# Branch D's gates as seven half-width products, convolution taps written behind weight chunks, an earlier layer norm and weight sums in four stretches

## The chip, the core and the metric

The kernel runs on one core of one Trainium2 chip. The metric is the device time of one execution in microseconds. A core has TensorE (PE, with its weight loads listed apart as PEld), VectorE (DVE), ScalarE (ACT), GpSimd (POOL) and SyncE (SP, which here only issues transfers); they run side by side and wait for one another through semaphores.

## The reference, cut to what matters

One layer over 512 time steps and 1024 channels, all in 32-bit floats. `h` is the normalised input; `z = h @ W_in` is cut into the inputs of four mixers and into four blocks of 1024 gate columns.

```python
y_sc   = (sc_b * causal_dwconv(sc_c * sc_x, sc_conv)) @ sc_out           # branch s
y_pool = pool_mixer(pool_in, pool_w, pool_scale)                         # branch p
y_conf = silu(layer_norm(causal_dwconv31(glu(conf_in)) + conf_b)) @ conf_out   # branch c
y_diff = diff_attention(q, k, v, ...) @ diff_out                         # branch d
x = x + (sum of sigmoid(gate_i) * y_i) @ w_o
x = x + conv_glu_ffn(rms_norm(x))                                        # 1024 -> 2 x 2816 -> 1024
```

`causal_dwconv31` is a depthwise convolution with 31 taps over 512 channels.

## The kernel before, in words

Activations lie channel-major: a tile holds 128 channels by 512 time steps. Every 32-bit operand is split into a high and a low part of the type fp32r, and a product is three matmuls: high by high, high by low, low by high (`mm3`). One 128x128 weight block with its three matmuls of 512 columns is a "unit".

**Weights** come in one stream of chunks through three buffers each of `raw`, `whi` and `wlo`. A plain chunk ("n" in `PLAN`) holds eight blocks, 128x1024; for each, SP issues one transfer, ACT casts the high part (L156) and DVE subtracts to get the low part (L157). `step` calls `load_chunk` for up to two chunks ahead of the one that the matmuls read. `state["unit"]` counts units; `at(u, f)` and `after(d, f)` run `f` when the count reaches a due unit, which places its instructions in the program order at that point. A planner then orders each engine's queue, except where `manual_schedule` keeps the order of the program; for POOL that holds throughout.

**Seven products** (`seven`, `products`): a 2x2 grid of weight blocks is multiplied by a pair of activation blocks with seven products of 256 columns in place of eight (each three matmuls). One such group of blocks takes a chunk of kind "s": three plain blocks from `wa` and four sums of blocks from `sums`, 896 columns in all, in two transfers. The sums are made on the fly by POOL's accumulating transfers in DRAM (`make_sums`, four transfers for each group of four chunks, each waiting for the one before). The activation side is prepared by `fold`, once per pair of channel tiles. Four PSUM banks hold the results; two ACT copies and four DVE adds turn them into the outputs (L702 to L715).

**Order of the work.** The convolution's inputs (chunks 0 to 7), q, k, v (8 to 19), branch s's and p's inputs with attention between them as timed events, then s outputs and gates, p outputs and gates (up to chunk 56). Branch d then has for each of eight tiles an output product (`mixed`, 4 units, tile `yd`) and a gate (`gate`, 8 units, tile `gtd`): the first four (`STD = 4`), then the four gate pairs of branch c in seven products each (tiles `gc0` to `gc6`, kept in `gates`), then the other four. Branch c's outputs (`yc`) follow with their merges, then `w_o`, then the feed-forward layer in two parts: ten up-projected tiles and a down projection in seven products (`dn0x`), then twelve and another (`dn1x`).

The 124 taps (L402, L405, tile `cacc`) are events spread from 32 to 560 units after the first time-major product. The layer norm (`norm_mean`, `norm_center` `MULAG` units later, `norm_out` `VARLAG` units after that) begins before the last gate pair of branch c. The weight sums come in three calls: groups 0 to 2 with k's heads, 3 to 6 after the pool inputs, 7 to 14 after the last gate of branch c.

Of the kernel before, what the change touches and what calls it, by code (L numbers as in the profile page):

```python
# [9 lines left out]
F32 = mybir.dt.float32  # L10
# [23 lines left out]
UPC = CW // P  # L34
AHEAD = 2
STEP = 13
TAP0 = 32
TAP1 = 560
VLAG = 8
OLAG = 13  # L40
WARM = 8
# [4 lines left out]
SW = 4 * P  # L46
SUMU = 30
EARLY = 3
MIDDLE = 7
DEEP = 2  # L50
ENDS = 3
STD = 4
FOLD = 4
FOLDS = 14
FOLD0 = -26
MULAG = 22
VARLAG = 14
PLAN = [("n", 57 + 3 * STD // 2)]
PLAN += [("s", MP * FOLD), ("n", 3 * (KD - STD) // 2 + 4 + 8 + 2 * CUT), ("s", MP * CUT // 2), ("n", 2 * (NP - CUT)), ("s", MP * (NP - CUT) // 2)]
LOG_EXP = "natural_log_exp_and_others"  # L60
START = 2
PIECES = 4
PLAG = 20
NLAG = 11
ALAG = 6
HP = 0
SQ0 = 8
NTMP = 12
SQS = 4
# [20 lines left out]
def hybrid_layer_kernel(ctx: ExitStack, tc: tile.TileContext, xT: bass.AP, w: bass.AP, cols: bass.AP, wa: bass.AP,  # L90
# [12 lines left out]
    def bank(name):  # L103
        return psum.tile([P, T], F32, tag="bank", name=name)

    def t2(name, dt=F32):
        return tmp.tile([P, TW], dt, tag="tmp", name=name)[:, :T]

    def m2(name, dt=F32R):
        return mid.tile([P, T], dt, tag="mid", name=name)  # L110
# [11 lines left out]
    sums = [dram.tile([P, GRP * SW], F32, name=f"sums{g}") for g in range(n_of["s"] // GRP)]  # L122

    fetched = []

    def fetch(i, pieces=1):
        kind, c = plan[i]
        raw = wp.tile([P, CW], F32, tag="raw", name=f"wr{i}", bufs=3)
        if kind == "s":
            g, o = divmod(c, GRP)  # L130
            n = AW + SW
            nc.sync.dma_start(raw[:, :AW], wa[c])
            nc.sync.dma_start(raw[:, AW:n], sums[g][:, o * SW:(o + 1) * SW])
            return ((slice(0, n), raw[:, :n]),)
        cuts = [slice(i * CW // pieces, (i + 1) * CW // pieces) for i in range(pieces)]
        for s in cuts:
            nc.sync.dma_start(raw[:, s], w[c][:, s])
            if pieces > 1 and s.start == 0:
                nc.sync.dma_start(xt[0], xT[0])
        return tuple((s, raw[:, s]) for s in cuts)  # L140

    def load_chunk(pieces=1, between=None):
        c = len(chunks)
        while len(fetched) <= min(c + (DEEP if plan[c][0] == "s" else 0), len(plan) - 1):
            if len(fetched) > c and plan[len(fetched)][0] == "n":
                break
            fetched.append(fetch(len(fetched)))
        hi = wp.tile([P, CW], F32R, tag="whi", name=f"wh{c}", bufs=3)
        lo = wp.tile([P, CW], F32R, tag="wlo", name=f"wl{c}", bufs=3)
        with tc.high_priority(HP):  # L150
            for cut, raw in fetched[c]:
                n = (cut.stop - cut.start) // pieces
                for i in range(pieces):
                    s = slice(cut.start + i * n, cut.start + (i + 1) * n)
                    src = raw[:, i * n:(i + 1) * n]
                    nc.scalar.copy(hi[:, s], src)  # L156
                    nc.vector.tensor_tensor(out=lo[:, s], in0=src, in1=hi[:, s].bitcast(F32), op=ALU.subtract)  # L157
                if between and cut.start == 0:
                    between()
        chunks.append((hi, lo))  # L160

    events = []
# [2 lines left out]
    def at(u, f):  # L165
        events.append((u, len(events), f))
        events.sort(key=lambda e: e[:2])
# [89 lines left out]
    def col(name, i=0, n=1):  # L257
        o = COLS[name] + i
        return gains[:, o:o + n] if o < NG else colt[:, o - NG:o - NG + n]
# [9 lines left out]
    def raw_in(k):  # L269
        raw.append(split(xt[k], f"raw{k}", scale=col("mix_norm", k)))  # L270

    nc.scalar.dma_start(gains, cols[:, :NG])
    fetched.append(fetch(0, PIECES))
    nc.scalar.dma_start(xt[1], xT[1])
    fetched.append(fetch(1))
# [68 lines left out]
    def conf_glu(j, pa, pg):  # L344
# [3 lines left out]
        nc.vector.tensor_tensor(out=g, in0=g, in1=rs, op=ALU.mult)  # L348
        nc.vector.tensor_tensor(out=glus[j][:, CK - 1:], in0=pa, in1=g, op=ALU.mult)

    first = [bank(f"ca{i}") for i in range(4)]
    def input_norm():
        ps = bank("ss1")
# [38 lines left out]
        conf_glu(j, pa, pg)  # L392
    for k in range(KD):
        after(NLAG * k, lambda k=k: norm(k))

    acc31 = [None] * 4

    def tap(j, i):
        wc = col("conf_conv", j * CK + i)
        if i == 0:  # L400
            acc31[j] = m2(f"cacc{j}", F32)
            nc.vector.tensor_scalar(  # L402
                out=acc31[j], in0=glus[j][:, :T], scalar1=wc, scalar2=col("conf_b", j), op0=ALU.mult, op1=ALU.add)
        else:
            nc.vector.scalar_tensor_tensor(  # L405
                out=acc31[j], in0=glus[j][:, i:i + T], scalar=wc, in1=acc31[j], op0=ALU.mult, op1=ALU.add)

    def time_major(name):
        pss = [bank(f"{name}{t}") for t in range(4)]
# [51 lines left out]
    nc.vector.tensor_reduce(out=lam2, in_=lamt, op=ALU.add, axis=AX.X)  # L461
    lam = const.tile([P, 1], F32, name="lamc")

    taps = [(j, i) for j in range(4) for i in range(CK)]
    u1, u2 = state["unit"] + TAP0, state["unit"] + TAP1
    for n, (j, i) in enumerate(taps):
        at(u1 + (u2 - u1) * n // len(taps), lambda j=j, i=i: tap(j, i))
    qrows = qk_norm("q", time_major("q"))
    qT, kT = [], []
    after(QLAG, lambda: qT.extend(qk_heads("q", qrows, qg)))  # L470
# [244 lines left out]
        nc.vector.tensor_tensor(out=s5_, in0=p2[:, :H], in1=s5_, op=ALU.add)  # L715
        return p1[:, H:], p3[:, H:], p3[:, :H], s5_

    def gate_pair(m, name, keep=False):
        c11, c12, n21, n22 = seven(f"g{name}{m}", hops)
        gs = [m2(f"sg{name}{m + i}", F32) if keep else t2(f"sg{name}{m + i}") for i in range(2)]  # L720
        for g, c, x, scale in (
                (gs[0], right, c11, 1.0), (gs[0], left, c12, 1.0), (gs[1], right, n21, -1.0), (gs[1], left, n22, -1.0)):
            nc.scalar.activation(g[:, c], x, AF.Sigmoid, scale=scale)
        return gs

    def gate(m, name, keep=False):
        pg = bank(f"gt{name}{m}")
        project(pg, h)
        g = m2(f"sg{name}{m}", F32) if keep else t2(f"sg{name}{m}")
        nc.scalar.activation(g, pg, AF.Sigmoid)  # L730
        return g

# [13 lines left out]
    def mixed(m, name, act):  # L746
        py = bank(f"y{name}{m}")
        project(py, act)
        return py
# [7 lines left out]
        py = mixed(m, "p", [ypool[m // 2]])  # L757
        merge(m, py, gate(m, "p"), scale=col("pool_scale", m))
    ydiff = [(od[0][:, i, :], od[1][:, i, :]) for i in range(HEADS)]
    for m in range(STD):  # L760
        py = mixed(m, "d", ydiff)
        merge(m, py, gate(m, "d"))
    yconf = []
    gates = []

    def norm_mean():
        t = t2("cm")
        nc.vector.tensor_tensor(out=t, in0=acc31[0], in1=acc31[1], op=ALU.add)
        for j in (2, 3):
            nc.vector.tensor_tensor(out=t, in0=t, in1=acc31[j], op=ALU.add)  # L770
        after(MULAG, lambda a=tsplit(t, "mu"): norm_center(a))
# [14 lines left out]
            nc.scalar.activation(a, a, AF.Silu, scale=col("ln_g", j), bias=col("ln_b", j))  # L786
            yconf.append(split(a, f"yc{j}"))

    for m in range(0, KD, 2):
        if m == KD - 2:  # L790
            while events:
                events.pop(0)[2]()
            norm_mean()
        gates += gate_pair(m, "c", True)
    turn = sm.tile([P, 1], F32, tag="turn", name="turn", bufs=1)
    nc.gpsimd.tensor_copy(turn, gates[-1][:, :1])
    make_sums(MIDDLE, len(sums))
    for m in range(STD, KD):
        py = mixed(m, "d", ydiff)
        merge(m, py, gate(m, "d"))  # L800
    for m in range(KD):
        merge(m, mixed(m, "c", yconf), gates[m], last=True)

    x1 = []
    for m in range(KD):
# [60 lines left out]

    parts = ((0, CUT), (CUT, NP))
    for part, (p0, p1) in enumerate(parts):
        ops, free, even = [], list(homes), None
        last = [hs[:, k, j, :] for k in range(KD) for j in (0, 1)]  # L870
        for p in range(p0, p1):
            g = ffn_up(p)
            if p % 2:
                ops.append(operands(p // 2, even, g, last if p == NP - 1 else free))
            even = g
        for m in range(MP):
            y0, y1 = x1[2 * m], x1[2 * m + 1]
            o0, o1 = (y0, y1) if part == 0 else (t2(f"outa{m}"), t2(f"outb{m}"))
            if part and m == MP - 1:
                seven_last(f"dn{part}{m}", ops, y0, y1, o0, o1,  # L880
                           lambda i, c, q: q.dma_start(out[2 * m + i][:, c], (o0, o1)[i][:, c]))
                continue
            c11, c12, n21, n22 = seven(f"dn{part}{m}", ops)
            for o, y, c, z, op in (
                (o0, y0, right, c11, ALU.add), (o0, y0, left, c12, ALU.add),
                (o1, y1, right, n21, ALU.subtract), (o1, y1, left, n22, ALU.subtract)):
                nc.vector.tensor_tensor(out=o[:, c], in0=y[:, c], in1=z, op=op)
            if part:
                for i, o in enumerate((o0, o1)):
                    for c in (right, left):  # L890
                        nc.sync.dma_start(out[2 * m + i][:, c], o[:, c])


def _layout(x, mix_norm, w_in, sc_conv, sc_out, pool_w, pool_scale, conf_conv, conf_conv_b, conf_ln_g, conf_ln_b,
# [39 lines left out]
    for m in range(KD):  # L934
        parts.append(pw[m // 2][:, (m % 2) * P:(m % 2 + 1) * P])
        gate_of(1, m)
    for m in range(STD):
        tile_of(do, m)
        gate_of(3, m)
    for m in range(STD, KD):  # L940
        tile_of(do, m)
        gate_of(3, m)
    for m in range(KD):
        tile_of(co, m)
    for m in range(KD):
# [4 lines left out]
    stream = np.concatenate(parts, axis=1)  # L950
    w = np.ascontiguousarray(stream.reshape(P, -1, CW).transpose(1, 0, 2))

    pairs = [(win, 36 + 2 * 8 + m, k) for m in range(0, KD, 2) for k in range(FOLD)]
    for k0, k1 in ((0, CUT // 2), (CUT // 2, NP // 2)):
        pairs += [(dn, m, k) for m in range(0, KD, 2) for k in range(k0, k1)]

# [53 lines left out]
```

## Time and profile before

| | |
|---|---|
| median of 3 runs | 877.63 us (876.4 to 877.92) |
| profiled execution | 875.85 us, of which 874.1 us is the span from the first to the last instruction |
| TensorE | 4514 matmuls, busy 868.5 us (99%), granted clock 0.999 |
| VectorE | 686.3 us (79%) |
| ScalarE | 415.7 us (48%) |
| transfers | 143.68 MB, 164 GB/s on the mean |

Busy time is the time covered by an engine's instructions. Matmuls are pipelined and overlap in the records, so the pace of TensorE is read from the distance between starts.

### The profile page before, as it was taken

The numbers are of one execution on the slowest core, as the hardware profiler recorded it, in microseconds if no ns is written. First come the engines' busy times: TensorE is split into PE (matmuls) and PEld (weight loads), VectorE is DVE, ScalarE is ACT, GpSimd is POOL, SyncE is SP. The second block draws the span as 40 slices with busy tenths as digits, with TensorE's granted clock in tenths as the row PEclk, the third lists the DMA queues.
The fourth block names the chain that finished last, engine by engine and source line by source line (L and its number), as shares of the span: only waits on it lengthen the run. The fifth ranks groups of instructions, "written<-read, shape, count | busy, mean of one in ns | idle before, by whom it ended". The sixth has DMA issues, their size and how long they took to land.

```text
span 874.1 us, 12008 instructions
## 1 busy us (share of the span) xinstructions
PE 868.5 (99%) x4514; PEld 742.4 (85%) x4514; DVE 686.3 (79%) x1099; ACT 415.7 (48%) x624; POOL 85.9 (10%) x114
## 2 busy tenths in 40 slices
PE   9999999999999999999999999999999999999998
PEld 7888888888888888899888888888899888888998
DVE  7299976897867997998778566988876788888856
ACT  7243355464666434335574345444454344444532
POOL 1003301102411100000011011111000000000000
PEclk9999999999999999999999999999999999999999
DMA  7333377762398784347779887879876422223573
GB/s 263 112 97 97 121 180 207 183 142 97 126 223 199 177 201 123 111 125 210 208 195 244 214 207 210 216 212 208 172 198 188 125 101 97 97 99 88 160 227 119
DMA packets 64842, 143.68 MB, mean 164 GB/s; under 512 B 5536, under 2 KB 31136, under 8 KB 64544
## 3 DMA queue, kind: packets, MB, share of 16 engines
q1 hardware_dynamic: 40112, 99.26, 35.0%
q0 software_dynamic: 24240, 43.26, 25.3%
q8 instruction: 35, 0.57, 0.3%
q10 hardware_dynamic: 432, 0.40, 0.1%
q14 instruction: 23, 0.19, 0.1%
HBM read 140.80 MB, written 45.35 MB: 213 GB/s over the span
## 4 chain that ended last, share of the span: by engine, by line
PE 97%; DVE 1%; DMA 1%; issue 0%; ACT 0%; SPq 0%; DVEq 0%
PE fg L197 14%; PE fu L197 14%; PE gts L197 5%; PE gtd L197 5%; PE wo L197 5%; PE gtp L197 5%; PE c L197 3%; PE pi L197 3%; PE x L197 3%; PE ys L197 3%; PE k L197 2%; PE yd L197 2%; PE b L197 2%; PE v L197 2%; PE yc L197 2%; PE q L197 2%
## 5 line engine op out<-in xcount | busy, mean ns | idle before, releaser
L156 ACT CAST wh<-wr 128x1024 fp32r<-128x1024 f32 (+2 forms) x189 | 188.2, 998 | 231.6 <-issue 30.1
L157 DVE TENSOR_TENSOR wl<-wr,wh 128x1024 fp32r<-128x1024 f32 (+2 forms) x189 | 219.6, 1165 | 68.8 <-ACT wh L156 61.5
L197 PE MATMUL fg<-hs,wh 128*128 128x512 f32 x352 | 108.4, 389 | 0.0
L197 PE MATMUL fu<-hs,wh 128*128 128x512 f32 x352 | 108.4, 389 | 0.0
L405 DVE SCALAR_TENSOR_TENSOR cacc<-glu,colt,cacc 128x512 f32<-128x512 f32 x120 | 89.8, 748 | 2.3
L197 PEld LDWEIGHTS fu<-hs,wh 128*128 128x128 f32 x352 | 66.1, 188 | 13.8
L197 PEld LDWEIGHTS fg<-hs,wh 128*128 128x128 f32 x352 | 66.0, 188 | 13.7
L830 DVE SCALAR_TENSOR_TENSOR fc<-f,colt,fc 128x512 f32<-128x512 f32 x88 | 65.8, 749 | 7.4 <-ACT fc L828 6.3
L197 PE MATMUL fg<-hs,wl 128*128 128x512 f32 x176 | 68.5, 389 | 0.0
L197 PE MATMUL fu<-hs,wl 128*128 128x512 f32 x176 | 68.5, 389 | 0.0
L828 ACT ACTIVATE fc<-f,colt 128x512 f32<-128x512 f32 x44 | 31.6, 718 | 19.1 <-DVE f L114 16.6
L197 PE MATMUL gts<-hs,wh 128*128 128x512 f32 x128 | 40.0, 394 | 0.0
L197 PE MATMUL gtd<-hs,wh 128*128 128x512 f32 x128 | 39.4, 389 | 0.0
L197 PE MATMUL gtp<-hs,wh 128*128 128x512 f32 x128 | 39.4, 389 | 0.0
L197 PEld LDWEIGHTS fg<-hs,wl 128*128 128x128 f32 x176 | 33.0, 188 | 6.8
L197 PEld LDWEIGHTS fu<-hs,wl 128*128 128x128 f32 x176 | 33.1, 188 | 6.8
L825 DVE TENSOR_TENSOR f<-fu,rs 128x512 f32<-128x512 f32 x22 | 15.1, 688 | 20.3 <-PE fu L197 20.3
L242 POOL DMA_DIRECT2D sums<-s x15 | 15.2, 1013 | 141.1 <-DMA sums<-s 141.1
L197 PEld LDWEIGHTS gts<-hs,wh 128*128 128x128 f32 x128 | 23.7, 188 | 5.5 <-issue 0.7
L197 PEld LDWEIGHTS gtd<-hs,wh 128*128 128x128 f32 x128 | 24.0, 188 | 5.0
L197 PEld LDWEIGHTS gtp<-hs,wh 128*128 128x128 f32 x128 | 24.0, 188 | 5.0
L505 ACT ACTIVATE p<-p,st 128x128 f32<-128x128 f32 (+3 forms) x32 | 17.7, 555 | 16.9 <-DVE st L502 16.8
(1685 smaller groups left out, 2131.6 us busy)
## 6 DMA issues: line engine op xcount, KB each, us to landing
wr<-w SPq DMA_DIRECT2D x124, 512.0 KB, 3.6
sums<-s POOLq DMA_DIRECT2D x15, 1024.0 KB, 9.5
wr<-sums SPq DMA_DIRECT2D x60, 256.0 KB, 3.8
wr<-wa SPq DMA_DIRECT2D x60, 192.0 KB, 3.0
sums<-s POOLq DMA_DIRECT2D x15, 512.0 KB, 7.0
sums<-s POOLq DMA_DIRECT2D x15, 256.0 KB, 4.8
x<-xT SPq DMA_DIRECT2D x8, 256.0 KB, 3.8
xin<-xT SPq DMA_DIRECT2D x1, 1024.0 KB, 8.1
```

What stands on the lines that cost most here:

```text
L156: nc.scalar.copy(hi[:, s], src)
L157: nc.vector.tensor_tensor(out=lo[:, s], in0=src, in1=hi[:, s].bitcast(F32), op=ALU.subtract)
L197: nc.tensor.matmul(ps, a[i], b[j], start=start and n == 0, stop=stop and n == 2, skip_group_check=shared)
L242: lambda g: nc.gpsimd.dma_start(view(g, 2, 4), src(s2, g, 2), accum_op=ALU.add),
L405: nc.vector.scalar_tensor_tensor(out=acc31[j], in0=glus[j][:, i:i + T], scalar=wc, in1=acc31[j], op0=ALU.mult, op1=ALU.add)
L505: nc.scalar.activation(p[:, :n], p[:, :n], AF.Exp, bias=st[:, m:m + 1], scale=-1.0, accum_out=st[:, 2 + m:3 + m])
L825: nc.vector.tensor_tensor(out=u[:, 2:2 + T], in0=ps, in1=rs, op=ALU.mult)
L828: nc.scalar.activation(c, u[:, 2:2 + T], AF.Copy, scale=col("ffn_conv", o + 2))
L830: nc.vector.scalar_tensor_tensor(out=c, in0=u[:, i:i + T], scalar=col("ffn_conv", o + i), in1=c, op0=ALU.mult, op1=ALU.add)
```

## The change

Branch d's eight gates are computed by `gate_pair` as branch c's are, four pairs in seven products each; `hops`, the folded activations, serve both. For each pair of tiles of d and then of c, the order is now: gate pair, two output products, two merges. `STD`, the kept gates and their eight tiles are gone. The plan has 76 "s" chunks (60 before) and 117 "n" chunks (125 before), so 19 groups of sums (15 before).

The taps are no longer events: `load_chunk` for chunks 9 to 50 runs under `manual_schedule` on DVE and appends `TAPS[c]` taps behind the chunk's low part. The folds are due 38 units earlier. `norm_mean` is called once the pool branch's products are written, ahead of branch d. Weight sums: groups 0 to 2 and 3 to 7 where the first two calls were, 8 to 12 after the last merge of branch c, 13 to 18 when the first down projection has written `x1[7]`. At the start, the small `gains` transfer and the first input tile swap their queues.

```diff
-TAP0 = 32
-TAP1 = 560
...
-MIDDLE = 7
+MIDDLE = 8
+LATE = 13
...
-STD = 4
...
-FOLD0 = -26
+FOLD0 = -64
...
-PLAN = [("n", 57 + 3 * STD // 2)]
-PLAN += [("s", MP * FOLD), ("n", 3 * (KD - STD) // 2 + 4 + 8 + 2 * CUT), ("s", MP * CUT // 2), ("n", 2 * (NP - CUT)), ("s", MP * (NP - CUT) // 2)]
+PLAN = [("n", 57)] + 2 * MP * [("s", FOLD), ("n", 1)]
+PLAN += [("n", 8 + 2 * CUT), ("s", MP * CUT // 2), ("n", 2 * (NP - CUT)), ("s", MP * (NP - CUT) // 2)]
+TAPS = dict(zip(range(9, 51), (
+    5, 0, 4, 6, 3, 0, 2, 6, 1, 0, 4, 1, 2, 2, 4, 2, 4, 2, 3, 5, 5, 3, 3, 2, 3, 4, 3, 3, 5, 0, 0, 0, 2, 4, 5, 2, 2, 4, 4,
+    6, 5, 3)))
...
             if pieces > 1 and s.start == 0:
-                nc.sync.dma_start(xt[0], xT[0])
+                nc.sync.dma_start(gains, cols[:, :NG])
...
-        with tc.high_priority(HP):
+        with ExitStack() as order:
+            if c in TAPS:
+                order.enter_context(tc.manual_schedule(engines={mybir.EngineType.DVE}))
...
+            for _ in range(TAPS.get(c, 0)):
+                tap(*taps.pop(0))
...
-    nc.scalar.dma_start(gains, cols[:, :NG])
+    nc.scalar.dma_start(xt[0], xT[0])
...
-    u1, u2 = state["unit"] + TAP0, state["unit"] + TAP1
-    for n, (j, i) in enumerate(taps):
-        at(u1 + (u2 - u1) * n // len(taps), lambda j=j, i=i: tap(j, i))
...
-    for m in range(STD):
-        py = mixed(m, "d", ydiff)
-        merge(m, py, gate(m, "d"))
...
-    for m in range(0, KD, 2):
-        if m == KD - 2:
-            while events:
-                events.pop(0)[2]()
-            norm_mean()
-        gates += gate_pair(m, "c", True)
-    turn = sm.tile([P, 1], F32, tag="turn", name="turn", bufs=1)
-    nc.gpsimd.tensor_copy(turn, gates[-1][:, :1])
-    make_sums(MIDDLE, len(sums))
-    for m in range(STD, KD):
-        py = mixed(m, "d", ydiff)
-        merge(m, py, gate(m, "d"))
-    for m in range(KD):
-        merge(m, mixed(m, "c", yconf), gates[m], last=True)
+    norm_mean()
+
+    def more_sums(x, g0, g1):
+        turn = sm.tile([P, 1], F32, tag="turn", name=f"turn{g0}", bufs=1)
+        nc.gpsimd.tensor_copy(turn, x[:, :1])
+        make_sums(g0, g1)
+
+    for name, act in (("d", ydiff), ("c", yconf)):
+        for m in range(0, KD, 2):
+            gs = gate_pair(m, name)
+            for i in (m, m + 1):
+                merge(i, mixed(i, name, act), gs[i - m], last=name == "c")
+    more_sums(merged[-1][0].bitcast(F32), MIDDLE, LATE)
...
     for part, (p0, p1) in enumerate(parts):
+        if part:
+            more_sums(x1[KD - 1], LATE, len(sums))
...
-    pairs = [(win, 36 + 2 * 8 + m, k) for m in range(0, KD, 2) for k in range(FOLD)]
+    pairs = [(win, 36 + br * 8 + m, k) for br in (3, 2) for m in range(0, KD, 2) for k in range(FOLD)]
```

## Rows read from the trace of the kernel before

**Rows 1.** The page: busy time, share and instructions of each engine; chain by engine.
```profile
PE 868.5 (99%) x4514; PEld 742.4 (85%) x4514; DVE 686.3 (79%) x1099; ACT 415.7 (48%) x624; POOL 85.9 (10%) x114
PE 97%; DVE 1%; DMA 1%; issue 0%; ACT 0%; SPq 0%; DVEq 0%
```
**Rows 2.** All waits of TensorE in the span: us, times, longest.
```profile
PE warm L282 <- DVE zeros L279: 1.5, 1, 1.5
PE ca L197 <- ACT raw0h L224: 0.5, 1, 0.5
```
**Rows 3.** Timeline of TensorE: start us, length us, engine, line, operation, tiles, count.
```profile
358.37 0.62 PE L197 MATMUL gtd<-hs,wh 128*128 128x512 f32 x2
...
363.81 0.62 PE L197 MATMUL yd<-od,wh 128*128 128x512 f32 x2
...
380.13 0.40 PE L197 MATMUL gc0b<-at,wh 128*128 128x256 f32 x2
...
390.20 0.40 PE L197 MATMUL gc2b<-at,wh 128*128 128x256 f32 x2
```
**Rows 4.** Windows: length; busy us (instructions) of PE, PEld, DVE, ACT, POOL; clock; DMA.
```profile
46.46:138.54 92.08, 92.08 (x433) 76.45 (x431) 80.27 (x131) 39.88 (x62) 18.85 (x13) 1.00 0.48 138
138.54:247.37 108.83, 108.83 (x537) 88.44 (x535) 92.94 (x187) 61.98 (x118) 23.25 (x24) 1.00 0.58 151
247.37:303.97 56.60, 56.60 (x267) 46.82 (x266) 41.22 (x68) 30.70 (x50) 7.30 (x9) 1.00 0.83 198
379.98:420.28 40.30, 40.30 (x337) 40.26 (x336) 36.20 (x49) 22.72 (x38) 0.00 (x0) 1.00 0.61 183
```
**Rows 5.** Windows of the taps alone (L405): length, DVE busy (instructions), clock, DMA.
```profile
46.46:138.54 92.08, 22.49 (x30) 1.00 0.48 138
138.54:247.37 108.83, 22.37 (x30) 1.00 0.58 151
247.37:303.97 56.60, 15.30 (x21) 1.00 0.83 198
```
**Rows 6.** Groups of instructions by line and shape: count, busy us, mean ns, idle before.
```profile
L157 DVE TENSOR_TENSOR wl<-wr,wh 128x1024 fp32r<-128x1024 f32 x123 | 151.7, 1234 | 39.4 <-ACT wh L156 32.6 <-PE ss L336 6.3
L157 DVE TENSOR_TENSOR wl<-wr,wh 128x896 fp32r<-128x896 f32 x60 | 65.1, 1089 | 26.3 <-ACT wh L156 25.8
L714 DVE TENSOR_TENSOR gc0r<-gc0c,gc0q 128x512 f32<-128x512 f32 x1 | 0.7, 685 | 0.0
```
**Rows 7.** Timeline of ScalarE in the layer norm.
```profile
435.97 0.69 ACT L315 ACTIVATE rlv<-var,epsc 128x512 f32<-128x512 f32 x1 [2.86 <-PE var L337]
...
443.16 1.05 ACT L156 CAST wh<-wr 128x1024 fp32r<-128x1024 f32 x1 [1.18 <-PE gtd L197]
...
452.34 1.05 ACT L156 CAST wh<-wr 128x1024 fp32r<-128x1024 f32 x1
```
**Rows 8.** Timeline of POOL: first, 29th and last of the third call's 32 transfers.
```profile
424.73 0.53 POOL L240 DMA_DIRECT2D sums<-s  x1
...
607.24 0.90 POOL L240 DMA_DIRECT2D sums<-s  x1
...
634.50 1.01 POOL L243 DMA_DIRECT2D sums<-s  x1 [8.06 <-DMA sums<-s]
```
**Rows 9.** Timelines of DVE and SP: `x1[7]` after `dn0`; the last group's first fetch.
```profile
682.14 0.42 DVE L887 TENSOR_TENSOR x<-x,dn03s 128x256 f32<-128x256 f32 x1
...
850.07 0.32 SPq L133 DMA_DIRECT2D wr<-sums  x1
```
**Rows 10.** The page, transfers: count, size, median us from issue to landing.
```profile
wr<-sums SPq DMA_DIRECT2D x60, 256.0 KB, 3.8
...
sums<-s POOLq DMA_DIRECT2D x15, 256.0 KB, 4.8
```
**Rows 11.** Timeline of ScalarE at the start.
```profile
4.92 0.72 ACT L224 ACTIVATE raw0h<-xin,gains 128x512 fp32r<-128x512 f32 x1 [1.11 <-DMA xin<-xT]
...
8.17 1.14 ACT L156 CAST wh<-wr 128x512 fp32r<-128x512 f32 x2 [0.97 <-DMA wr<-w]
```

More of the change, by code (lines that the diff above doesn't have):

```diff
@@ L65 @@
 ALAG = 6
-HP = 0
 SQ0 = 8
@@ L124, in hybrid_layer_kernel @@
     fetched = []
+    taps = []
     def fetch(i, pieces=1):
@@ L349, in conf_glu, with tap @@
         nc.vector.tensor_tensor(out=glus[j][:, CK - 1:], in0=pa, in1=g, op=ALU.mult)
+    acc31 = [None] * 4
+    def tap(j, i):
+        wc = col("conf_conv", j * CK + i)
+        if i == 0:
+            acc31[j] = m2(f"cacc{j}", F32)
+            nc.vector.tensor_scalar(
+                out=acc31[j], in0=glus[j][:, :T], scalar1=wc, scalar2=col("conf_b", j), op0=ALU.mult, op1=ALU.add)
+        else:
+            nc.vector.scalar_tensor_tensor(
+                out=acc31[j], in0=glus[j][:, i:i + T], scalar=wc, in1=acc31[j], op0=ALU.mult, op1=ALU.add)
+    taps += [(j, i) for j in range(4) for i in range(CK)]
     first = [bank(f"ca{i}") for i in range(4)]
@@ L394, in hybrid_layer_kernel @@
         after(NLAG * k, lambda k=k: norm(k))
[L396 to L406, printed above, removed]
     def time_major(name):
@@ L462, in hybrid_layer_kernel @@
     lam = const.tile([P, 1], F32, name="lamc")
-    taps = [(j, i) for j in range(4) for i in range(CK)]
-    u1, u2 = state["unit"] + TAP0, state["unit"] + TAP1
-    for n, (j, i) in enumerate(taps):
-        at(u1 + (u2 - u1) * n // len(taps), lambda j=j, i=i: tap(j, i))
     qrows = qk_norm("q", time_major("q"))
@@ L716, in seven, with gate_pair @@
         return p1[:, H:], p3[:, H:], p3[:, :H], s5_
-    def gate_pair(m, name, keep=False):
+    def gate_pair(m, name):
         c11, c12, n21, n22 = seven(f"g{name}{m}", hops)
-        gs = [m2(f"sg{name}{m + i}", F32) if keep else t2(f"sg{name}{m + i}") for i in range(2)]
+        gs = [t2(f"sg{name}{m + i}") for i in range(2)]
         for g, c, x, scale in (
@@ L724, in gate_pair, with gate @@
         return gs
-    def gate(m, name, keep=False):
+    def gate(m, name):
         pg = bank(f"gt{name}{m}")
         project(pg, h)
-        g = m2(f"sg{name}{m}", F32) if keep else t2(f"sg{name}{m}")
+        g = t2(f"sg{name}{m}")
         nc.scalar.activation(g, pg, AF.Sigmoid)
@@ L759, in hybrid_layer_kernel @@
     ydiff = [(od[0][:, i, :], od[1][:, i, :]) for i in range(HEADS)]
-    for m in range(STD):
-        py = mixed(m, "d", ydiff)
-        merge(m, py, gate(m, "d"))
     yconf = []
-    gates = []
     def norm_mean():
@@ L936, in _layout @@
         gate_of(1, m)
-    for m in range(STD):
+    for m in range(KD):
         tile_of(do, m)
[L939 to L942, printed above, removed]
     for m in range(KD):
```

## The prediction

> **What bounds the kernel now.** I read the page first: TensorE is busy 99% of the span and 97% of the chain that ended last is TensorE [rows 1]. Busy time alone proves little for a pipelined engine, so I read its waits next. In the whole span TensorE waits for another engine twice, both times in the first six microseconds [rows 2]. The reader should see that no wait is left to remove: only fewer or shorter matmuls can make this kernel faster, and any new wait makes it slower at full price. The timeline then gives the two paces. One gate of 24 matmuls of 512 columns runs from 358.37 to 363.81, 5.44 us, so 0.2267 us a matmul. One pair in seven products, 84 matmuls of 256 columns, runs from 380.13 to 390.20, 10.07 us, so 0.120 us a matmul [rows 3]. The windows show the clock at 1.00 throughout, its 2.4 GHz level, and how full the other engines are while TensorE never pauses [rows 4].
>
> **The matmuls.** Four pairs of branch d's gates change form. A pair cost 2 x 5.44 = 10.88 us and will cost 10.07 us [rows 3]: 0.81 us saved, 3.24 us for four. The saving is small because the matmul count rises from 48 to 84 and half the columns cost 53% of the time. The `yd` and `yc` products, the two layer norm sums and everything else on TensorE are only reordered. This term is exact as long as the pace of the `gc` stage holds when two plain products follow each pair.
>
> One rule speaks against this term. The Trainium skill, page "TensorE: Matmul & The Clock Gate", section "Back-to-back issue gap", puts a sustained stream of weight load and matmul at about 81 ns for 128 columns and 131 ns for 512. A straight line between them, an estimate, gives 98 ns for 256, hence 84 x 98 = 8.2 us against 48 x 131 = 6.3 us a pair: four pairs would lose 7.8 us instead of gaining 3.2. This trace does not agree, with 227 and 120 ns in this kernel's own type, and I go by the rows.
>
> **The weights.** Eight plain chunks become sixteen of kind "s". VectorE has 16 x 1.089 - 8 x 1.234 = 7.6 us more to subtract [rows 6], ScalarE a similar amount to cast, SP 24 more transfers to issue. Each pair also gets an epilogue, about 3 x 0.685 + 0.42 = 2.5 us of VectorE. What hides it: branch c's four pairs, back to back, leave VectorE 36.20 of 40.30 us busy and ScalarE 22.72, taps among it, without a wait of TensorE [rows 2, 4]. In the new order a pair with its two plain products lasts 10.07 + 5.44 = 15.5 us, and VectorE needs in it 4 x 1.089 + 1.234 + 2.5 + four merge operations at about 0.685 = 10.8 us. Price 0; without that cover each microsecond VectorE falls behind, past the two chunks of lead, is one of TensorE's.
>
> **The taps.** All 124 now sit behind chunks 9 to 50. A chunk is loaded when the matmuls reach the one two before it, so I map `TAPS` on the windows: 42 fall in 46 to 139 us, 47 in 139 to 247, 35 in 247 to 304. Now there are 30, 30 and 21 (and one first tap in each, of L402, which I leave as it is); VectorE does 57.8, 70.6 and 25.9 us without them [rows 4, 5]. With 41, 46 and 34 at 22.49 / 30 = 0.75 us the new load is 88.5 of 92.1, 105.1 of 108.8 and 51.4 of 56.6 us. It fits, with 3% to 9% to spare. What is queued behind a tap is the next chunk's low part, for which TensorE waits. From 304 us on VectorE has no taps at all, which makes room for the earlier folds. Bounds: 0, and 4.3 us if VectorE's operations come out 6% longer in the first two windows (193.6 x 0.06 = 11.6 us, of which 7.3 are to spare). I take 0, since the sums stay under the time in all three.
>
> **The layer norm.** `norm_mean` moves ahead of branch d. `norm_center` falls 22 units later, at the end of the first pair; `norm_out` runs at the first step 14 units after that, the plain products of the second pair. Branch d begins 10.88 us (two products of 2.72, one gate) before 358.37 [rows 3], at 347.5, so that is about 347.5 + 15.5 + 10.1 = 373 us. Before, that work fell on plain chunks of 5.44 us each. There ScalarE needed from 435.97 past 452 us for the norm, and between two weight casts 9.2 us went by, from 443.16 to 452.34 [rows 7]. Now this stretch runs into the third pair's seven products, where a chunk lasts 10.07 / 4 = 2.52 us and two chunks of lead are 5.0 us. Bounds: 0 if the planner slips the casts between the activations, 9.2 - 5.0 = 4.1 us if the casts stay as far apart. I take 0.3 us, nearer to nothing: the windows show that this engine has spare time in such a stage (22.72 of 40.30 us, [rows 4]), and branch c does not need the norm until its first output product, at 347.5 + 4 x 15.5 + 10.1 = 420 us.
>
> **The weight sums.** Four more groups, 16 POOL transfers. The second call now makes five groups in place of four, and nothing behind it on POOL is urgent. The third call, after the merges at 347.5 + 8 x 15.5 = 471.5, makes five by 471.5 + 5 x 26.1 = 602 (pitch below), and the first down projection begins eight `w_o` products and ten tiles later, at 471.5 + 28 x 5.44 = 624. The fourth is the close one. Six groups start when `x1[7]` is written, 682.56 before [rows 9], 679.3 with 3.24 us saved. Seven groups took 607.24 - 424.73 = 182.5 us, 26.1 us each, and the eighth took 634.50 - 607.24 plus a landing of 4.8, 32 us [rows 8, 10]. So the last of six lands at about 679.3 + 5 x 26.1 + 32.1 = 842 us. Its first chunk, fourth from the end of the 24, is fetched at 850.07 - 3.2 = 846.8 [rows 9]. SP issues in order, so a late group holds back every fetch and store behind it. The margin is 5 us, and what the two chunks ahead in the buffers give beyond it. Price 0, bounds 0 to 8 us (each of the five groups 10% slower, 13 us, less the margin).
>
> By the Trainium skill, page "DMA: Bandwidth & Descriptors", section "Anatomy of one DMA", a POOL transfer takes 2 us plus its bytes at 436 GB/s: an estimate of 15 us for a group, and no danger at all. The rows show 26, so I keep the risk.
>
> **The start.** The first matmul waits for `raw0h`, which waited 1.11 us for its input [rows 11]; its transfer now goes first on ACT's queue. That can bring at most 1.1 us, or cost some tenths if `gains`, now second on SP, is late. But ScalarE's next casts wait for a later weight transfer at 8.17 [rows 11], which sits behind the same bytes as before, and the matmuls catch up with them. I take 0, bounds -0.5 to +0.3.
>
> **The sum.** The profiled execution took 875.85 us (span 874.1 and 1.75 around it): -3.24 + 0.3 gives 872.9. The median of the runs was 877.63, 1.78 above the profiled one; the same difference gives 874.7. About 0.2%, 1.75 us, is what a measurement of this kernel can tell from no change.
>
> **The rivals.** (1) The forecast: the matmuls are saved and no wait of weight comes in, 874.7; chance 0.56. (2) The norm's burst starves the third pair: TensorE waits 1.5 to 4 us near 380 to 395 us, 877.63 - 3.2 + 2.5 = 876.9, most often no measurable change; for it the 9.2 us gap, against it the idle ScalarE in rows 4; 0.23. (3) The slower one: the last weight sum arrives late, TensorE stops in the last pair of the second down projection. It decides from a landing at about 852 us on (the fetch at 846.8 and two chunks of 2.52 us), and the kernel is slower than before by 0.2% when the wait passes 3.24 + 1.75 = 5 us, that is at 857, or a group pitch of 29.1 in place of 26.1 us. Those groups run beside the stores and a faster weight stream at the end, which speaks for it; the price is 5 to 8 us, 879.4 to 882.4; 0.10. (4) The pinned taps push a chunk's low part past its use somewhere from 50 to 250 us: 1.5 to 5 us, 876 to 879.5; the sums at 96% speak for it, against it that they fit; 0.09. (5) The change does not do what it says, because weight loads set the pace of narrow products: PEld is busy 40.26 of 40.30 us in the `gc` stage. At the 76.45 / 431 = 0.177 us that a load is busy beside wide matmuls [rows 4], 84 would take 14.9 us, 4 x 4.0 us more than two plain gates, and 893.6; as the stage kept 0.120 us, 0.02. The spacing of the Trainium skill's page quoted above ("TensorE: Matmul & The Clock Gate", "Back-to-back issue gap") would give 877.63 + 7.8 = 885.4 for the same reason.
>
> **How the numbers follow.** Faster comes from (1) and 0.02 of (2): 0.58. Same: 0.18 of (2), 0.02 of (3), 0.05 of (4): 0.25. Slower: 0.03 of (2), 0.08 of (3), 0.04 of (4), 0.02 of (5): 0.17. The range starts at 873.4, which is the full 3.24 with one more microsecond from the start and the runs' spread (877.63 - 3.24 - 1.0), and ends at 879.5, past (2) and most of (4), leaving out (5) and most of (3). If (1) holds, its own range is 873.4 to 875.8.
>
> **What would show it.** In the new trace: tiles `gd0` to `gd6` with 10.07 us from one start to 84 matmuls later; branches d and c together 3.2 us shorter; no wait of TensorE longer than 0.3 us after the first 20 us. It is wrong if TensorE waits for the casts or low parts near the third `gd` pair, for `wr<-sums` in `dn13`, or in 50 to 250 us.

## The result and the profile after

The changed kernel takes 885.79 us (median of 4 runs, 884.33 to 886.98) against 877.32 us of the kernel before on the same chip (4 runs, 876.4 to 877.92). The ratio is 1.0097, 95% interval 1.0077 to 1.0117: slower, outside the range and on the other side of the forecast. Its profiled execution took 884.33 us, with a span of 882.6.

The page, lines that answer to [rows 1]:

```profile
PE 869.1 (98%) x4658; PEld 747.5 (85%) x4658; DVE 702.6 (80%) x1123; ACT 424.4 (48%) x647; POOL 102.5 (12%) x131
...
PE 88%; DMA 5%; DVE 5%; issue 1%; ACT 1%; SPq 0%; DVEq 0%; ACTq 0%; POOL 0%
```

TensorE's busy time has barely moved, since a wait doesn't count as busy and the matmuls became more and narrower. The chain tells more: transfers and VectorE now hold 5% of it each, where they held 1%. All waits of TensorE in the new span, to be read against [rows 2]:

```profile
PE gd2d L202 <- DVE wl L160: 2.5, 1, 2.5
PE dn11d L202 <- DVE wl L160: 1.6, 3, 0.6
PE warm L287 <- DVE zeros L284: 1.5, 1, 1.5
PE dn11d L202 <- ACT wh L159: 1.2, 2, 0.9
PE dn12d L202 <- DVE wl L160: 1.0, 2, 0.6
PE dn12d L202 <- ACT wh L159: 0.8, 1, 0.8
PE sc L497 <- DVE at L227: 0.5, 1, 0.5
PE dn11b L202 <- DVE wl L160: 0.3, 1, 0.3
PE ca L202 <- ACT raw0h L229: 0.2, 1, 0.2
```

Three new places: the second gate pair of branch d, the second and third pairs of the second down projection, and the attention scores. The printed waits of `dn11` and `dn12` add up to 4.9 us; from start to start the same places lose 7.4 us against the pace of 0.120 us a matmul, so the printed waits understate the loss. Comparing the first matmul of each tile in the two traces puts the 8.5 us between the spans into five stretches:

| stretch | before | after | change |
|---|---|---|---|
| to the start of `pa` | 28.26 | 28.66 | +0.40 |
| from there to branch d | 319.23 | 320.12 | +0.89 |
| branches d and c, to the first `wo` | 128.34 | 128.02 | -0.32 |
| from `wo` to `dn10` | 333.78 | 333.82 | +0.04 |
| `dn10` to the end | 64.45 | 71.94 | +7.49 |

The new matmuls do what was forecast. TensorE's timeline, first matmuls of the first pair, of the products behind it, of the second pair and its wait, and of the third pair (compare [rows 3]):

```profile
348.78 0.40 PE L202 MATMUL gd0b<-at,wh 128*128 128x256 f32 x2
...
358.85 0.63 PE L202 MATMUL yd<-od,wh 128*128 128x512 f32 x2
...
364.79 0.40 PE L202 MATMUL gd2b<-at,wh 128*128 128x256 f32 x2
...
369.82 0.40 PE L202 MATMUL gd2d<-hs,wh 128*128 128x256 f32 x2
372.72 0.39 PE L202 MATMUL gd2d<-hs,wl 128*128 128x256 f32 x1 [2.50 <-DVE wl L160]
...
383.56 0.40 PE L202 MATMUL gd4b<-at,wh 128*128 128x256 f32 x2
```

The first pair takes 10.07 us. The second has a hole from 370.22, the end of two matmuls, to 372.72, in which TensorE wants the low part of its third chunk. VectorE's timeline shows what stood ahead of that low part:

```profile
366.79 2.48 DVE L775 SCALAR_TENSOR_TENSOR cacc<-mu,cacc 128x512 f32<-128x512 f32 x4
369.18 0.68 DVE L739 TENSOR_TENSOR sgd<-yd,sgd 128x512 f32<-128x512 f32 x1
369.78 0.68 DVE L292 TENSOR_TENSOR total<-total,cv 128x512 f32<-128x512 f32 x1
370.38 0.68 DVE L745 TENSOR_TENSOR acc<-acc,sgd 128x512 f32<-128x512 f32 x1
370.98 0.68 DVE L292 TENSOR_TENSOR total<-total,cv 128x512 f32<-128x512 f32 x1
371.58 1.08 DVE L160 TENSOR_TENSOR wl<-wr,wh 128x896 fp32r<-128x896 f32 x1
```

That is `norm_center` (L775 and the squares' sums of L292) and the two operations of one merge (L739, L745). The chunk's fetch had landed at 362.82; on ScalarE its cast stood behind the first square of `norm_center` and ended at 368.97.

For the second down projection the transfers in a window tell most. First the kernel before, from 812 to 852 us: packets, MB, share of the 16 DMA engines by queue, then fetches and median us to landing (q1 is the hardware queue of SP's fetches, q0 the software queue of POOL's sums):

```profile
q1 hardware_dynamic: 5647, 8.20, 71.8%
...
wr<-sums SPq DMA_DIRECT2D x16, 256.0 KB, 3.9
```

The same window after:

```profile
q1 hardware_dynamic: 3897, 5.82, 49.4%
q0 software_dynamic: 2263, 3.25, 44.1%
...
wr<-sums SPq DMA_DIRECT2D x12, 256.0 KB, 6.2
```

Undisturbed, the weight stream takes 71.8% of the DMA engines. The sums of the fourth call take 44.1%; the two don't fit together. The fetches get 49.4%, a fetch takes 6.2 us instead of 3.9, and 12 chunks come in the time of 16.

### The profile page after: what moved, and what is told of

Its sections match the earlier page's. It is cut to its first block, busy times and chain, and to the rows that moved or that the text cites. A ratio compares the mean times of both kernels' runs of the same rounds, so it can differ in the third digit from the quotient of the medians.

```text
span 882.6 us, 12445 instructions
## 1 busy us (share of the span) xinstructions
PE 869.1 (98%) x4658; PEld 747.5 (85%) x4658; DVE 702.6 (80%) x1123; ACT 424.4 (48%) x647; POOL 102.5 (12%) x131
## 4 chain that ended last, share of the span: by engine, by line
PE 88%; DMA 5%; DVE 5%; issue 1%; ACT 1%; SPq 0%; DVEq 0%; ACTq 0%; POOL 0%
PE fg L202 14%; PE fu L202 14%; PE gts L202 5%; PE wo L202 5%; PE gtp L202 5%; DMA wr<-sums 3%; PE c L202 3%; PE x L202 2%; PE yc L202 2%; PE v L202 2%; PE b L202 2%; PE k L202 2%; PE q L202 2%; PE ys L202 2%; PE pi L202 2%; PE yd L202 2%
## 5 line engine op out<-in xcount | busy, mean ns | idle before, releaser
L159 ACT CAST wh<-wr 128x1024 fp32r<-128x1024 f32 (+3 forms) x197 | 194.7, 991 | 232.3 <-DMA wr<-sums 41.9
L160 DVE TENSOR_TENSOR wl<-wr,wh 128x1024 fp32r<-128x1024 f32 (+3 forms) x197 | 227.1, 1156 | 76.7 <-ACT wh L159 69.4
L365 DVE SCALAR_TENSOR_TENSOR cacc<-glu,colt,cacc 128x512 f32<-128x512 f32 x120 | 92.1, 768 | 1.8
L247 POOL DMA_DIRECT2D sums<-s x19 | 19.3, 1014 | 177.9 <-DMA sums<-s 177.9
L246 POOL DMA_DIRECT2D sums<-s x19 | 19.5, 1024 | 127.6 <-DMA sums<-s 127.6
L248 POOL DMA_DIRECT2D sums<-s x19 | 19.2, 1011 | 124.5 <-DMA sums<-s 118.0
```

The costliest lines, as they stand in the source:

```text
L246: lambda g: nc.gpsimd.dma_start(sums[g], s1[g], accum_op=ALU.add, max_dma_last_dim=GRP * SW),
L247: lambda g: nc.gpsimd.dma_start(view(g, 2, 4), src(s2, g, 2), accum_op=ALU.add),
L248: lambda g: nc.gpsimd.dma_start(view(g, 3, 4), src(s3, g, 1), accum_op=ALU.add))
L365: nc.vector.scalar_tensor_tensor(out=acc31[j], in0=glus[j][:, i:i + T], scalar=wc, in1=acc31[j], op0=ALU.mult, op1=ALU.add)
```

## The experiments

The first theory, from these rows: two separate losses, the traffic of the sums beside the second down projection (7.5 us) and `norm_center` ahead of a low part in branch d (some 3 us). Rivals: a last group that lands late, and a loss that the new order of VectorE's work makes wherever the norm stands. Each experiment was timed beside the kernel before, whose median lay between 875.89 and 877.32 us, so the ratios compare better than the medians. `e1` to `e3` differ from the changed kernel in how many sums run when, `e4` in the norm.

**One group of sums moved from the fourth call to the third.**

```diff
-LATE = 13
+LATE = 14
```

> Six weight-sum groups in the third call and five in the fourth, instead of five and six. Theory 'traffic' (weight-sum transfers in flight slow every fetch of a seven-product stage, whose low parts are ready only 2 to 3 us ahead): the last group lands near 826 us instead of 852, so the second down projection loses 0 to 2 us instead of 7.5, the first one gets about 17 us of overlap and loses at most 1; total 5 to 7 us less, 879 to 881 us. Theory 'order' (the new order of the engine queues in the second down projection is at fault, not the transfers): the 7.5 us stay, 885.8.

Measured: 879.69 us, ratio 1.0032 (1.0016 to 1.0048), span 877.9. The last group landed at 819.94, `dn10` to the end took 64.56 us, and the waits of `dn1` are gone:

```profile
PE gd2d L202 <- DVE wl L160: 3.2, 1, 3.2
PE warm L287 <- DVE zeros L284: 1.5, 1, 1.5
PE dn00a L202 <- DVE wl L227: 0.6, 1, 0.6
PE sc L497 <- DVE at L227: 0.5, 1, 0.5
PE ca L202 <- ACT raw0h L229: 0.2, 1, 0.2
```

The price appears at the other end: the third call now reaches into the first down projection, and from the first matmul of `dn00` to that of `dn01` 13.47 us go by instead of 12.59 (13.35 and 12.47 to the last matmul of `dn00`).

**All late groups in the third call.**

```diff
-LATE = 13
+LATE = 19
```

> All eleven remaining groups in the third call, none in the fourth. 'Traffic': the transfers run from about 481 to 768 us, so the second down projection is clean (64.5 us from its first matmul to the end, as before the change) and the first one, overlapped in full, now loses 4 to 8 us; total 882 to 886 us. 'Order': the second down projection stays at 72 us and the first at 50.3 us.

Measured: 889.31 us, 1.0158 (1.0126 to 1.0189). `dn1` is clean at 64.54 us. From the first matmul of `dn00` to that of `dn10`, 10.5 us more go by than in the kernel before, with new waits up to 2.1 us in `dn01` to `dn03` and in the up projection behind them (`fg`): more than the 4 to 8 us expected. The loss goes where the sums go.

**The fourth call makes only the first of its four transfers** (its weights are then incomplete, three quarters of the additions are left out).

```diff
-            for f in steps:
+            for f in steps[:1] if g0 == LATE else steps:
```

> The fourth call makes only the first of the four transfers of each group (the three accumulating ones of groups 13 to 18 are left out, so the second down projection uses incomplete sums). 'Traffic': those groups are done near 730 us, the second down projection takes 64.5 us, total 878.3 us. 'Order': 72 us and 885.8 us as in the changed kernel.

Measured: 879.46 us, 1.0034 (1.0019 to 1.0049), `dn1` 64.55 us. Same call, TensorE, VectorE and ScalarE in the same order from `dn10` on, less traffic, no loss.

**The layer norm later.**

```diff
-MULAG = 22
-VARLAG = 14
+MULAG = 38
+VARLAG = 24
```

> The layer norm's second and third step due 38 and 24 units after their triggers instead of 22 and 14, so that both start in the plain products of a pair. Theory 'norm' for the 2.8 us wait at the second gate pair of branch d (the norm's operations stand ahead of that chunk's cast and low part): the wait goes, 2.5 to 3 us less, 883.0 us. Theory 'traffic' for the same wait (fetches of 6 us, because group 7 lands only at 364 us): 2 us or more of it stay, 885 us or more.

Measured: 881.3 us, 1.0054 (1.0039 to 1.0069), span 878.8, lower than the 883.0 expected. The wait in `gd2` is gone and the pair takes its 10 us (364.17 to 374.13); `dn10` to the end still takes 71.1:

```profile
PE dn11d L202 <- ACT wh L159: 2.8, 1, 2.8
PE warm L287 <- DVE zeros L284: 1.5, 1, 1.5
PE dn11d L202 <- DVE wl L160: 0.9, 2, 0.6
PE sc L497 <- DVE at L227: 0.5, 1, 0.5
PE ca L202 <- ACT raw0h L229: 0.2, 1, 0.2
```

The two losses are separate. The edit moves both later steps of the norm; that it was `norm_center` is read from the trace. Open is whether the norm made this wait alone: the second call's sums ran until 364.28 in the changed kernel, and a fetch of the second pair, issued at 354.28, took 6.3 us. Here they ran until 370.86 and no wait came, so the norm is needed for it; that the sums are not needed too, no run shows. The next five were built on each other, to see what is left.

**Both cures together** (LATE 14, MULAG 38, VARLAG 24).

> The changed kernel with both single cures together: LATE 14 (no group of sums beside the last down projection) and MULAG 38, VARLAG 24 (norm_center and norm_out later). Theory: the two losses are separate. LATE 14 alone had a span of 877.9, of which the second gate pair of branch d still held 5.3 us of wait and lowered clock (20.84 us to the third pair's start in place of 15.53). Without it the span is 877.9 - 5.3 = 872.6, the median about 1.8 above, 874.4, and the granted clock is 1.00 in every stretch of branch d. Rival: the norm's burst costs its 2 to 3 us wherever it is put, so that a wait of that length shows near a later pair, span 875 to 876 and a median near 877.5. Either way no wait in dn1.

Measured: 875.88 us, 0.9989 (0.9976 to 1.0001), span 875.2. Some 10 of 885.79 are back, but 2.6 us of the span fewer than expected. The theory was too clean: waits of 0.4 us (`gd2`), 0.8 (`gd4`) and 0.7 (`dn01`) for low parts remained, beside the 0.5 of the scores. The rival, a burst that costs its 2 to 3 us wherever it stands, had the span right, 875 to 876, but none of these waits is as long.

**The start put back**, on top of that: `gains` first on ACT's queue, `xt[0]` on SP's.

```diff
-                nc.sync.dma_start(gains, cols[:, :NG])
+                nc.sync.dma_start(xt[0], xT[0])
...
-    nc.scalar.dma_start(xt[0], xT[0])
+    nc.scalar.dma_start(gains, cols[:, :NG])
```

> The one before it, with the start as it was in the kernel before: gains first on ACT's queue, xt[0] behind the first piece of weights on SP's. Theory: the swap costs 0.4 us (ca ended at 28.44 instead of 28.03, pa began at 28.66 instead of 28.26), so the first matmul of pa comes at about 28.26 again and the whole is 0.4 us shorter than the one before it, near 874.0. Rival: the 0.4 us are chance of one execution; pa's start varies as much between runs of either order and the median does not move.

Measured: 877.16 us, 1.0003 (0.9993 to 1.0014), 1.3 us longer rather than 0.4 shorter. The theory fell. The profiled execution was the slowest of the 12, 879.21 us. In it TensorE's timeline shows the first product late, and the next ones 0.43 us apart instead of 0.23:

```profile
6.76 0.80 PE L202 MATMUL ca<-raw0h,wh 128*128 128x512 f32 x1 [1.52 <-ACT raw0h L229]
7.36 0.63 PE L202 MATMUL ca<-raw0h,wl 128*128 128x512 f32 x1
7.78 0.63 PE L202 MATMUL ca<-raw0h,wh 128*128 128x512 f32 x1
```

**Taps moved**, on top of that: five taken from behind chunks 36 and 37 and put behind 51 and 52.

```diff
-TAPS = dict(zip(range(9, 51), (
+TAPS = dict(zip(range(9, 53), (
...
-... 3, 3, 5, 0, 0, 0, 2, 4, 5, 2, 2, 4, 4, 6, 5, 3)))
+... 3, 1, 2, 0, 0, 0, 2, 4, 5, 2, 2, 4, 4, 6, 5, 3, 3, 2)))
```

> The one before it, with five taps taken from behind chunks 36 and 37 (3 to 1, 5 to 2) and put behind chunks 51 and 52. Theory: the wait of the scores' stage, 0.5 us of TensorE and 0.9 us from pi to ys and gts, came from pinned taps in front of the attention weights' low part (L227); with them gone from 213 to 226 us, gts begins 0.9 us earlier and the median is near 873.1. Rival: the slow stretch is made by the pool additions on GpSimd beside which VectorE runs slowly, taps or no taps, and the wait stays.

Measured: 877.09 us, 1.0003 (0.9988 to 1.0017). The wait for `at` is gone, and from `ys` to `gts` 4.73 us go by instead of 5.25; before it was 4.25. Half the loss is explained. Why the median didn't move is not shown: this profile has waits of 1.7 us in `gd0` and 0.5 in `gtp` that the one before it lacked, and lacks waits of 1.4 in `gd4`, 0.9 in `dn01` and 0.5 in `gd2` that the other had.

**The sums in five calls**, on top of that, meant to end the third before `dn00`.

```diff
-EARLY = 3
-MIDDLE = 8
+EARLY = 4
+MIDDLE = 9
...
         after(RLAG, spread_norm)
+        make_sums(0, 1)
...
-    after(QLAG + 1, lambda: make_sums(0, EARLY))
+    after(QLAG + 1, lambda: make_sums(1, EARLY))
```

> The one before it, with the weight sums spread so that no call overlaps a down projection: group 0 right after input_norm (some 36 to 64 us), groups 1 to 3 where 0 to 2 were, 4 to 8 where 3 to 7 were, 9 to 13 after the merges, 14 to 18 in the last call. Theory: overlap with the seven-product stages is what costs; dn00 goes back from 13.35 to 12.47 us, the median is 0.9 us shorter than the one before it, near 872.2. Rival: a group beside the first projections slows the fetches there and TensorE waits between 40 and 75 us, which takes the 0.9 us back or more.

Measured: 875.03 us, 0.998 (0.9966 to 0.9994), span 872.2: the median is 2.1 us shorter than the one before it. No wait of TensorE is left behind the first 20 us; the group at 36 to 64 us cost the first projections nothing. The 0.9 us expected at `dn00` are not what came back: in both profiles `dn00` to `dn01` takes 12.59 us. The spans differ by 4.1 us, all of it ahead of `wo`: the start, the wait in `gtp` and the one in `gd0`. Why those went with the sums' new places no run shows.

**The same with the changed kernel's start.**

> The version with the sums in five calls, the norm later and the taps moved, with the changed kernel's start (xt[0] first on ACT's queue, gains second on SP's). Theory, formed after the run that put the old start back and came out 1.3 us longer: the old order lets the first matmul wait up to 1.5 us for raw0h in some executions, after which TensorE runs at the lower clock level for some us; the new order avoids it. So this is 0 to 1.3 us shorter than the version with the old start: a median of 873.7 to 875.0, span 872.2 to 872.6. Rival: the old start costs the 0.4 us less that single traces showed, and this one comes out at 875.4.

Measured: 873.65 us (873.45 to 874.6), ratio 0.9971 (0.996 to 0.9983), span 871.8. This version beats both kernels, by 0.3% and some 1.3%. Its page and waits:

```profile
PE 866.3 (99%) x4658; PEld 747.4 (86%) x4658; DVE 701.8 (80%) x1123; ACT 428.0 (49%) x649; POOL 103.1 (12%) x131
...
PE 99%; DMA 0%; DVE 0%; ACT 0%; issue 0%; DVEq 0%; ACTq 0%
```

```profile
PE warm L287 <- DVE zeros L284: 1.5, 1, 1.5
PE ca L202 <- ACT raw0h L229: 0.4, 1, 0.4
```

**The kernel before with the new start alone** (the edit of the start the other way round).

> The kernel before with the changed start alone. The runs of the kernel before fall in two clusters, near 876.0 and near 877.6. Theory: the upper cluster are executions in which raw0h comes late and the clock falls for the first matmuls, and the new start takes it away: median 876.0, few runs above 876.8. Rival: the start is worth 0.4 us against it as in the first pair of traces, median 876.8 to 877.0, and both clusters stay.

Measured: 876.15 us, 0.9998 (0.9989 to 1.0007): no change of the median, which lies in the lower cluster either way. Beside it 6 of 22 runs of the kernel before were above 876.7 us; with the new start none of 11 was, which chance alone would give about once in 15. With the 35 runs beside `e5` to `e8` it is 23 of 57 against none of 11. In the six traces with the old start `pa` begins at 27.69 to 29.99 us, in the eight with the new one at 28.37 to 28.66. That the late first product of the old start makes the upper cluster fits, but is not shown: no run of the kernel before from that cluster was profiled.

**The kernel before with six groups of sums that nobody reads**, started where the changed kernel starts its fourth call.

```diff
     for part, (p0, p1) in enumerate(parts):
+        if part:
+            turn = sm.tile([P, 1], F32, tag="turn", name="turn2", bufs=1)
+            nc.gpsimd.tensor_copy(turn, x1[KD - 1][:, :1])
+            sums[:6] = [dram.tile([P, GRP * SW], F32, name=f"idle{g}") for g in range(6)]
+            make_sums(0, 6)
```

> The kernel before with six groups of sums that nobody reads, written to scratch memory from x1[7] on, where the changed kernel starts its fourth call. Nothing of the computation changes. Theory (traffic): the second down projection grows from 64.45 us by what it grew in the changed kernel, 7.5 us, give or take 2, and the median is 882 to 886; the granted DMA share beside it is above 0.9. Rival (something else of the change, the order of the instructions or the later weight chunks' numbers): it stays within 1 us of 64.45 and the median below 878.

Measured: 881.13 us, 1.0053 (1.004 to 1.0067); `dn10` to the end takes 69.61 us, 5.2 more. From 812 to 852 us:

```profile
q1 hardware_dynamic: 4480, 6.64, 51.8%
q0 software_dynamic: 1949, 3.05, 40.7%
...
wr<-sums SPq DMA_DIRECT2D x13, 256.0 KB, 5.7
```

The picture of the changed kernel without the change. The loss is smaller than expected (5.5 to 9.5 us, and a median of 882 to 886); its last group landed at 843.47 instead of 852.33.

**The same with plain copies** in place of the three accumulations of each group.

> As the one before it, with all four transfers of a group plain copies in place of one copy and three accumulations, over the same source bytes. If the accumulations' own cost per byte on the DMA engines makes the group last 26 us, the copies land well sooner (a pitch under 20 us, the last before 809) and the second down projection keeps its 64.45 us. If the bytes moved decide, the pitch stays near 26 us and the projection loses the same 5 to 9 us.

Measured: 876.4 us, 1.0003 (0.9993 to 1.0013). A group now takes 18.7 us ((777.54 - 684.12) / 5) instead of 25.3, the last landed at 800.66, and `dn1` takes 64.53 us. So it doesn't show what plain copies beside `dn1` would cost. What it does show is the price of a byte, from 740 to 780 us: first the groups with three accumulations of four transfers, then plain copies alone:

```profile
q0 software_dynamic: 2616, 4.41, 61.1%
```

```profile
q0 software_dynamic: 1293, 7.53, 53.2%
```

## Why the prediction was wrong

**The matmuls: right.** 10.07 us a pair; in the version without waits branches d and c take 125.29 us (348.23 to 473.52), 3.05 less than before, where 3.24 were forecast.

**The weight sums: the step that failed.** I asked only when the last group lands, and the chunk that needs it. It landed at 852.33, later than my 842: the call began at 685.08 instead of 679.3, its groups followed at the forecast 26.1 us, and the last took 36.9 us instead of 32.1. But its first fetch was issued at 859.42: the landing held nothing and there is no wait in `dn13`. That my bounds of 0 to 8 us hold the loss, and that rival (3) had about the right price, is luck: both were for a late landing. So is the nearness of the median to the 885.4 beside rival (5): the narrow products kept 0.120 us. What I left out is that a transfer in flight takes DMA time from the weight stream. [Rows 4] held half of the sum: in the `gc` stage, with no sums running, the DMA share was already 0.61. The other half stood beside it: from 247 to 304 us, where the second call ran, plain chunks and sums took 0.83, and the same trace has 0.30 and 0.38 from 340 to 380 us without sums against 0.78 from 420 to 460 with the third call, so the sums take 0.4 or more. I did not add the two. The term was 0, it measured 7.49. Shown by `e1` and `e3` (the loss goes with the traffic), `e2` (it follows it to `dn0`) and `e11` (it comes with traffic alone).

By the Trainium skill, page "DMA: Bandwidth & Descriptors", section "Issuing engines are not separate DMA queues", transfers run on the same 16 engines and interleave whoever issues them. The trace agrees: 44.1% and 49.4% add up to 93.5% of them. Another rule of the Trainium skill points elsewhere: page "Perfetto Trace Analysis", section "Identifying the Most-Contended Engine", advises the use of HBM utilization over occupancy for transfers. Here are windows of the last experiment, which has no wait there, and of the changed kernel, which waits (length, busy us of each engine, granted clock, DMA share, GB/s of the transfers, which stands in for the HBM's here):

```profile
740.00:780.00 40.00, 40.00 (x178) 33.10 (x178) 33.45 (x54) 18.38 (x26) 5.83 (x10) 1.00 0.81 281
```

```profile
825.00:845.00 20.00, 16.88 (x130) 15.65 (x129) 10.29 (x15) 6.36 (x9) 2.07 (x2) 1.00 0.94 216
```

The share tells them apart and the GB/s do not. The stages differ, though: the first is the up projection, where the weights alone took 0.28. In the down projection itself, from 825 to 845 us, the kernel before moved 214 GB/s at a share of 0.74 without a wait.

**The layer norm: the right burst, the wrong part of it, and too small.** I looked at `norm_out` on ScalarE near the third pair. The wait came from `norm_center` on VectorE at the second pair, 2.5 us against my 0.3, within the bounds. I had counted VectorE's load per pair and not the order in it: four subtractions, two sums and the two operations of a merge stood in front of one low part. The trace shows the order, and `e4` that without the norm there the wait goes.

**The taps: the sums were right, the place was not.** VectorE's load in the three windows came out at 86.5, 103.1 and 52.7 us, against my 88.5, 105.1 and 51.4. But a window of 109 us says nothing about 13 us of it: from 213 to 226 the kernel before ran no tap, now eight stood ahead of the scores' operands, two of them at 1.55 us beside POOL's additions (213.18 to 214.73, 218.85 to 222.23) instead of 0.74. The first and the last three on VectorE's timeline:

```profile
213.72 1.55 DVE L365 SCALAR_TENSOR_TENSOR cacc<-glu,colt,cacc 128x512 f32<-128x512 f32 x1
...
223.52 2.31 DVE L365 SCALAR_TENSOR_TENSOR cacc<-glu,colt,cacc 128x512 f32<-128x512 f32 x3
```

It cost 0.89 us; moving five taps gave 0.5 back, and the rest was not settled.

**The weights and the start: right in the end.** With the norm later and six groups in the third call, three versions still waited 0.4 to 1.7 us at a time for low parts in the first three pairs; in the two with the sums in five calls nothing waited for the sixteen chunks of kind "s". The start costs nothing measurable at the median; the +0.40 of the first trace lies within what single executions differ by.

## What to carry to other kernels

Before moving a background transfer, add its DMA share to that of the stage it will run beside, both read from windows of the trace. Here 0.61 beside the up projection's 0.28 cost nothing, and 0.44 beside the down projection's 0.72 cost 7.5 us while no landing was late. Room on an engine is read over the stretch between two uses, not over a stage: what counts is the work queued in front of the one operand that is wanted next. A change whose main term is right can still lose, and undoing one neighbour at a time gave it back here.

## What the runs showed of the hardware

A wait costs more than its length when the clock answers. In the run with the quartered sums TensorE waited 2.9 us in `gd2`, and `gd2` with the two products behind it took 21.83 us, 5.85 more than the 15.98 without the wait (`e4`); the windows at the end of that wait and behind it (length, busy us of each engine, granted clock, DMA share, GB/s):

```profile
372.00:374.00 2.00, 0.95 (x4) 0.96 (x5) 2.00 (x3) 1.01 (x2) 0.00 (x0) 0.59 0.00 0
374.00:376.00 2.00, 2.00 (x12) 2.00 (x11) 2.00 (x3) 0.25 (x1) 0.00 (x0) 0.50 0.83 226
376.00:378.00 2.00, 2.00 (x11) 2.00 (x11) 0.33 (x1) 0.00 (x0) 0.00 (x0) 0.50 0.87 259
378.00:380.00 2.00, 2.00 (x14) 2.00 (x14) 0.19 (x1) 1.21 (x2) 0.00 (x0) 0.71 0.63 199
```

0.50 is the 1.2 GHz level: matmuls of 256 columns start 0.213 us apart instead of 0.120. The 2.5 us wait of the changed kernel's profile left the clock at 1.00, but its three other runs had a mean clock of 0.994 to 0.996 and spans up to 885.2, which fits a fall of the clock in them; they have no trace. The windows may not show every slow stretch: from 6 to 10 us in the run with the start put back they print 1.00, with matmuls of 512 columns 0.43 us apart from 7.36 to 8.64.

Accumulating transfers from memory to memory cost the DMA engines more a byte than plain ones. Six groups moved the same 17.30 MB both ways: 54.6% of the 16 engines for 163 us with three accumulations a group, 40.6% for 121 us as plain copies, 1.8 times the engine time. In the 40 us shown, 61.1% for 4.41 MB against 53.2% for 7.53 MB, it is twice. An accumulation by itself was not timed apart.
